# Direct DMAs of a sliding-window copy: cut into 32 KB rows mostly while the staging ring loads, left at 64 KB rows mostly while it stores

## Chip, cores, metric

One core of one Trainium2 chip. The metric is device time in microseconds (us) of one execution; lower is better. Before the change: 752.56 us, the median of 3 runs (752.02 to 753.11).

## The reference

```python
batch, length, dim = (32, 4096, 256)          # x, float32
window_size, stride = 64, 32
n_windows = (length - window_size) // stride + 1        # 127
for i in range(n_windows):
    start = i * stride
    result[:, i] = x[:, start:start + window_size].copy()
```

This is a pure copy. A block of 32 rows of x is 32 KB. A window is two neighbouring blocks, 64 KB, and each block goes to two windows, once as second half and once as first half. The output is 266 MB.

## The kernel before

There are two ways to copy a batch, and each has its own DMA queue. *Direct* batches (21 of 32) go from DRAM to DRAM on the queue of the sync engine. *Staged* batches (11) are loaded into SBUF once and stored from there twice, on the queue of the scalar engine. A staged batch reads each byte of x once instead of twice, which spares the memory, but moves 12 MB through the DMA engines where a direct one moves 8.

```python
DIRECT, IN, OUT = 32768, 16384, 16384          # largest row of a DMA descriptor, bytes
# ... in class Copier:
    def windows(self, q, b, w0, n, half=None):     # n windows of batch b, whole or one half of each
        blk = self.blk                             # 8192 elements, 32 KB
        size = 2 * blk if half is None else blk
        off = blk if half else 0
        self.count(q.dma_start(
            out=self.oap((b * self.nw + w0) * 2 * blk + off, [[2 * blk, n], [1, size]]),
            in_=bass.AP(self.x.tensor, self.x.offset + (b * self.nb + w0) * blk + off,
                        [[blk, n], [1, size]]),
            max_dma_last_dim=DIRECT))
# ... in class Staging: 6 buffers; 6 loads, their 12 stores, 5 loads, their stores
    def run(self, q):
        bufs = len(self.tiles)
        for first in range(0, len(self.batches), bufs):
            group = range(first, min(first + bufs, len(self.batches)))
            for g in group:
                self.load(q, g)
            for g in group:
                self.store(q, g)
# ... in the kernel:
    staged = [*range(1, B - 3, 3), B - 2]
    direct = [b for b in range(B) if b not in staged]
    spilled = staged[:-1]      # their full stores also write one window of each neighbour batch
    def rest(b):               # that window and 14 more, again, after those stores ("repair")
        for n in (b - 1, b + 1):
            if n in spilled:
                st.wait_stored(ring_d, spilled.index(n))
        c.windows(ring_d, b, 0 if b - 1 in spilled else 112, 15)
    # ...
        late = 8
        for i, b in enumerate(direct):
            w0 = 15 if b - 1 in spilled else 0
            for j in range(7):
                if j % 3 == 1 or (j == 3 and i % 5 != 2):
                    c.windows(ring_d, b, w0 + 16 * j, 16, 0)     # "cut": two DMAs of 32 KB rows
                    c.windows(ring_d, b, w0 + 16 * j, 16, 1)
                else:
                    c.windows(ring_d, b, w0 + 16 * j, 16)        # "whole": one DMA of 64 KB rows
            if b in free:
                rest(b)
            elif i >= len(free) + late:
                rest(direct[i - late])
        for b in direct[-late:]:
            rest(b)
```

A "slot" below is one step of the loop over j: 16 windows, 1 MB. There are 147 slots, of which 59 are cut before the change. `free` holds the one direct batch (31) that has no spilled neighbour.

Of the kernel before, what the change touches and what calls it, by code (L numbers as in the profile page):

```python
# [1 line left out]

# [4 lines left out]


DIRECT, IN, OUT = 32768, 16384, 16384


class Copier:


    def __init__(self, nc, tc, x, out, B, L, D, W, S, n_win):
        assert W == 2 * S and L % S == 0
        self.nc, self.tc, self.x, self.out = nc, tc, x, out
        self.B = B
        self.blk = S * D
        self.nb = L // S  # L20
        self.nw = n_win
        self.total = 0
        self.done = tc.alloc_semaphore("done")

    def xap(self, block, dims):
        return bass.AP(self.x.tensor, self.x.offset + block * self.blk, dims)

    def oap(self, elem, dims):
        return bass.AP(self.out.tensor, self.out.offset + elem, dims)

    def count(self, dma):
        dma.then_inc(self.done, 16)
        self.total += 16

    def windows(self, q, b, w0, n, half=None):

        blk = self.blk
        size = 2 * blk if half is None else blk
        off = blk if half else 0
        self.count(  # L40
            q.dma_start(
                out=self.oap((b * self.nw + w0) * 2 * blk + off, [[2 * blk, n], [1, size]]),
                in_=bass.AP(
                    self.x.tensor,
                    self.x.offset + (b * self.nb + w0) * blk + off,
                    [[blk, n], [1, size]],
                ),
                max_dma_last_dim=DIRECT,
            )
        )  # L50

    def load(self, q, t, b):
        return q.dma_start(
            out=t[:, :], in_=self.xap(b * self.nb, [[self.blk, self.nb], [1, self.blk]]),
            max_dma_last_dim=IN,
        )

    def store(self, q, t, b, half, p0=0, n=None):



        blk = self.blk
        n = self.nb if n is None else n
        w = b * self.nw + p0 - half
        return q.dma_start(
            out=self.oap(w * 2 * blk + half * blk, [[2 * blk, n], [1, blk]]),
            in_=t[p0 : p0 + n, :],
            max_dma_last_dim=OUT,
        )


class Staging:


    def __init__(self, c, pool, dtype, batches, bufs):
        self.c, self.batches = c, batches
        self.tiles = [pool.tile([128, c.blk], dtype, name=f"xb{i}") for i in range(bufs)]
        self.loaded = [c.tc.alloc_semaphore(f"loaded{i}") for i in range(bufs)]
        self.stored = [c.tc.alloc_semaphore(f"stored{i}") for i in range(bufs)]

    def load(self, q, g):
        n, i = divmod(g, len(self.tiles))
        if n:
            q.wait_ge(self.stored[i], 32 * n)
        self.c.load(q, self.tiles[i], self.batches[g]).then_inc(self.loaded[i], 16)

    def store(self, q, g):
        n, i = divmod(g, len(self.tiles))
        q.wait_ge(self.loaded[i], 16 * (n + 1))
        if g == len(self.batches) - 1:  # L90

            for half, p0, rows in ((0, 0, 112), (0, 112, 15), (1, 1, 15), (1, 16, 112)):
                self.c.count(self.c.store(q, self.tiles[i], self.batches[g], half, p0, rows))
            return
        for half in (0, 1):
            self.c.store(q, self.tiles[i], self.batches[g], half).then_inc(self.stored[i], 16)

    def wait_stored(self, q, g):
        n, i = divmod(g, len(self.tiles))
        q.wait_ge(self.stored[i], 32 * (n + 1))  # L100
# [11 lines that stand above are left out]
@with_exitstack  # L112
def kernel(
    ctx: ExitStack,
    tc: tile.TileContext,
    x: bass.AP,
    window_size: bass.AP,
    stride: bass.AP,
    out: bass.AP,
):  # L120
    nc = tc.nc
    W, S = int(window_size), int(stride)
    B, L, D = x.shape
    n_win = (L - W) // S + 1
    assert out.shape == (B, n_win, W, D)
    c = Copier(nc, tc, x, out, B, L, D, W, S, n_win)
    staged = [*range(1, B - 3, 3), B - 2]
    direct = [b for b in range(B) if b not in staged]
    pool = ctx.enter_context(tc.tile_pool(name="xb", bufs=1))
    st = Staging(c, pool, x.dtype, staged, 6)  # L130
    ring_d, ring_s = nc.sync, nc.scalar
    spilled = staged[:-1]

    def rest(b):
# [6 lines that stand above are left out]
    with tc.tile_critical():  # L141
        st.run(ring_s)



        free = [b for b in direct if b - 1 not in spilled and b + 1 not in spilled]
        direct = free + [b for b in direct if b not in free]
        late = 8
        for i, b in enumerate(direct):
            w0 = 15 if b - 1 in spilled else 0  # L150
            for j in range(7):
                if j % 3 == 1 or (j == 3 and i % 5 != 2):
                    c.windows(ring_d, b, w0 + 16 * j, 16, 0)
                    c.windows(ring_d, b, w0 + 16 * j, 16, 1)
                else:
                    c.windows(ring_d, b, w0 + 16 * j, 16)
            if b in free:
                rest(b)
            elif i >= len(free) + late:
# [3 lines that stand above are left out]
        ring_d.wait_ge(c.done, c.total)  # L163


# [1 line left out]
_INS = ['x', 'window_size', 'stride']  # L167
_OUTS = [((32, 127, 64, 256), 'float32')]

_NUMBERS = {'window_size': 64, 'stride': 32}  # L170


# [26 lines left out]
```

## Time and profile before

| | before |
|---|---|
| median time | 752.56 us |
| span of the profiled run | 751.0 us |
| DMA engines busy, mean of 16 | 99.3% |
| moved by the DMA engines | 313.16 MB, 417 GB/s |
| memory read + written | 220.92 + 266.99 MB, 650 GB/s |

The page of the kernel before. The DMA line is the busy share in tenths of the 16 DMA engines in 40 equal slices of the span; the next line is the rate in those slices. Of the two queues, q1 is the direct one and q10 the staging one; the columns are packets, MB, and the time that their packets took as a share of 16 engines' span.

```profile
DMA  9999999999999999999999999999999999999996
GB/s 373 418 413 428 407 419 424 428 427 428 428 427 427 426 430 422 428 417 428 421 428 403 413 423 421 421 425 418 423 427 418 428 414 427 414 433 420 416 398 293
...
q1 hardware_dynamic: 8945, 174.80, 55.1%
q10 hardware_dynamic: 9002, 138.35, 44.2%
...
HBM read 220.92 MB, written 266.99 MB: 650 GB/s over the span
```

There is no compute to speak of and no idle time: 55.1% and 44.2% are 99.3% of all engines' time. When the engines are always busy, only three things can make the kernel faster: fewer bytes, packets that take less time, or no idle engine at the end.

The packet records of the trace say how long one transfer takes. This is a count over them, not a view of the profile. A completion is the 4-byte write by which one engine reports that its part of a DMA is done:

```
before            packets   median ns   sum per engine, us   above the median, us
q1, 32 KB            5334        1213                411.6                    7.2
q10, 16 KB           8444         611                331.6                    9.2
completions, 4 B     4169           9                  2.4                      -
```

Three quarters of the data packets take exactly the median, 27 bytes per ns on either queue, so I call it the floor. The last column is what packets slower than the floor cost an engine on average, called "excess" below: 16.4 of 751 us.

The waits of the sync queue (us in total, times, longest):

```profile
SPq L41 <- DMA out_dram<-xb: 56.0, 2, 41.5
```

These are the repairs, which wait for staging's stores. They cost nothing as long as the queue has work already issued.

### The profile page before, as it was taken

What the parts mean: (1) busy time and instruction counts of PE and PEld (TensorE: products, weight loads), DVE (VectorE), ACT (ScalarE), POOL (GpSimd) and SP (SyncE); (2) the same over time, 40 slices, a digit from 0 to 9 for tenths busy, and PEclk for the clock granted to TensorE, in tenths of its full rate; (3) what the DMA queues carried; (4) which work ended last, traced back from release to release, by engine and by line L of the source; (5) the groups of instructions that cost most, each with busy time, mean ns of one, the idle gap of its engine ahead of it and who ended that gap; (6) DMA issues with size and microseconds to landing.
All of it is one profiled execution on the core that took longest, in us unless ns stands there. A gap on an engine that the chain in (4) does not pass through costs nothing. (4 is left out here: it accounts for less than half of the span.)

```text
span 751.0 us, 312 instructions
## 1 busy us (share of the span) xinstructions
POOL 0.2 (0%) x4
## 2 busy tenths in 40 slices
POOL 0000000000000000000000000000000000000000
DMA  9999999999999999999999999999999999999996
GB/s 373 418 413 428 407 419 424 428 427 428 428 427 427 426 430 422 428 417 428 421 428 403 413 423 421 421 425 418 423 427 418 428 414 427 414 433 420 416 398 293
DMA packets 17949, 313.16 MB, mean 417 GB/s; under 512 B 4169, under 2 KB 4169, under 8 KB 4169
## 3 DMA queue, kind: packets, MB, share of 16 engines
q1 hardware_dynamic: 8945, 174.80, 55.1%
q10 hardware_dynamic: 9002, 138.35, 44.2%
q14 instruction: 2, 0.02, 0.0%
HBM read 220.92 MB, written 266.99 MB: 650 GB/s over the span
## 5 line engine op out<-in xcount | busy, mean ns | idle before, releaser
L180 POOL MEMSET const-bfloat16-1.0<- 128x1 bf16 x1 | 0.1, 102 | 0.0
L180 POOL MEMSET const-uint8-127<- 128x1 uint8 x1 | 0.1, 102 | 0.0
L180 POOL MEMSET const-float32-1.0<- 128x1 f32 x1 | 0.1, 99 | 0.0
L180 POOL MEMSET const-float32-0.0<- 128x1 f32 x1 | 0.1, 98 | 0.2 <-issue 0.2
## 6 DMA issues: line engine op xcount, KB each, us to landing
out_dram<-in_x_dram SPq DMA_DIRECT2D x88, 1024.0 KB, 95.8
out_dram<-xb ACTq DMA_DIRECT2D x20, 4096.0 KB, 138.5
out_dram<-in_x_dram SPq DMA_DIRECT2D x118, 512.0 KB, 95.0
xb<-in_x_dram ACTq DMA_DIRECT2D x11, 4096.0 KB, 133.6
out_dram<-in_x_dram SPq DMA_DIRECT2D x21, 960.0 KB, 96.3
out_dram<-xb ACTq DMA_DIRECT2D x2, 3584.0 KB, 96.7
out_dram<-xb ACTq DMA_DIRECT2D x2, 480.0 KB, 96.4
```

The costliest lines, as they stand in the source:

```text
L180: nc = _bacc.Bacc("TRN2", target_bir_lowering=False, num_devices=1)
```

## The change

The diff spreads the cuts unevenly. It counts "turns" (packets and completions of the direct queue on one engine) to estimate what the staging ring is doing. Of the slots that meet loads it cuts 5 in 6, of the others 1 in 6.

```diff
--- before.py
+++ after.py
@@ -146,14 +146,21 @@
         free = [b for b in direct if b - 1 not in spilled and b + 1 not in spilled]
         direct = free + [b for b in direct if b not in free]
         late = 8
+        share = turns = 0
         for i, b in enumerate(direct):
             w0 = 15 if b - 1 in spilled else 0
             for j in range(7):
-                if j % 3 == 1 or (j == 3 and i % 5 != 2):
+                loading = turns < 102 or 306 <= turns < 391
+                share += 5 if loading else 1
+                cut = share >= 6
+                turns += 4 if cut else 3
+                if cut:
+                    share -= 6
                     c.windows(ring_d, b, w0 + 16 * j, 16, 0)
                     c.windows(ring_d, b, w0 + 16 * j, 16, 1)
                 else:
                     c.windows(ring_d, b, w0 + 16 * j, 16)
+            turns += 3 if b in free or i >= len(free) + late else 0
             if b in free:
                 rest(b)
             elif i >= len(free) + late:
```

The intent: where the two queues alternate, a cut slot brings one completion more and with it one more turn for staging. So loads should get through faster beside cut rows, and the direct queue should catch up while staging stores. The changed kernel has 55 cut and 92 whole slots.

## The prediction

> **What bounds the kernel now.** No compute: the page lists four memsets, 0.2 us. Its 40 slices show the DMA engines at 9 tenths or more until the last slice (6 tenths). In its queue part, the direct queue (q1, DRAM to DRAM) takes 55.1% and the staging queue (q10, loads to SBUF and stores from it) 44.2% of 16 engines' span: 99.3%. Packet records of the trace: direct rows of 64 KB and of 32 KB all travel as 32 KB packets, median 1213 ns (5334 of them); staging packets are 16 KB, median 611 ns (8444); a completion write takes 9 ns. That is 27.0 and 26.8 bytes per ns: a byte has one price on both queues. Sums per engine: 411.6 + 331.6 us and 2.4 us of completions. The 15-row DMAs miss one engine (21 x 2 packets x 1.213 = 51 us), so the other 15 are busy 745.7 + 51/16 = 748.9 us of the 749.3 at which the last packet ends: no idle time to win. Only 16 us per engine lie above the floor (every packet at its median): packets slowed by contention.
>
> **What the change does.** Bytes, data packets and each engine's share stay. The queues seem to alternate packet by packet on an engine, a completion write being a turn: an uncut window DMA is 3 turns, a cut pair 4. Cutting only sets how many staging packets pass per direct megabyte. Before, 59 of 147 slots are cut, spread evenly; after, 55 (built order), 5 in 6 while staging loads, 1 in 6 while it stores. Removed: 4 completions, 0.04 us. Turns stay balanced (563 before, 559 after, staging about 549). Moved: loads get a larger share (the sixth landed at 137 us; I expect near 129), stores a smaller one, so the refill starts at nearly the old time.
>
> **Waits.** The sync queue waits twice for spilled stores before repair DMAs (waits view: 56.0 us, longest 41.5). With stores slower late, I expect 55 to 65 us, longest about 47. Some 95 us of work lies in the ring (issue to landing 95.8 us), so it doesn't run dry; if it did, staging alone would fill the engines: its first packets, alone, follow each other at 616 ns.
>
> **Critical path.** The engines' total work is the path, and none of it is removed. What can move is contention: staging's part is densest while loads run (3.3 of its 9.2 us in the first 125 us, more from 400 to 525). More cut rows beside loads may move this by 1 to 3 us either way. The Trainium skill, "DMA: Bandwidth & Descriptors", section "Issuing engines are not separate DMA queues", says that DMAs from several engines run on the same 16 and interleave; this trace agrees (two queues, 99.3%).
>
> **Predicted:** 752.0 us, 748 to 756 in 8 of 10; faster by over 2%: 0.02; within 2%: 0.95; slower by over 2%: 0.03.
>
> **Right or wrong would show in:** packet medians 1213 and 611 ns unchanged; queue shares 55 and 44%; the direct queue's rate lower during loads, higher during stores; the sixth load landing earlier; last direct packet near 749 us.
>
> **What would make it wrong:** 32 KB rows at 64 KB pitch contending more with loads than whole rows do; the direct queue running dry in a repair wait while staging also waits; arbitration that isn't turn by turn, so that the queues' ends separate and a tail on one queue runs slower.

## More of the kernel before

The views by stretch give the last column in GB/s and the DMA share before it (a packet is counted where it starts, so 1.01 can occur). The stretches are chosen after the staging ring: it loads in 25 to 125 and 425 to 525 us, and stores in 125 to 400 and 525 to 650.

```profile
25.00:125.00 100.00, 0.00 (x0) 1.00 1.01 420
125.00:400.00 275.00, 0.00 (x0) 1.00 1.01 425
425.00:525.00 100.00, 0.00 (x0) 1.00 1.00 420
525.00:650.00 125.00, 0.00 (x0) 1.00 1.01 422
730.00:740.00 10.00, 0.00 (x0) 1.00 0.93 401
```

Near the end the share is 0.93, close to 15/16: one engine seems to have finished, since the 21 DMAs of 15 rows use only 15 engines (the direct queue has 3611 completions, 227 x 16 less 21). The others stay busy to about 745 us.

## The result

The changed kernel took 752.62 us (median of 4, 751.76 to 753.78), the kernel before 752.84 in the same rounds (median of 4, 752.02 to 754.57). The ratio is 0.9995 with a 95% interval of 0.9972 to 1.0018: the same. Ratios here are the mean time of one kernel's fast runs over that of the other's of the same rounds, so not quite the ratio of the quoted medians. The kernel before differed from call to call (near 745 us in some, 753 to 755 in others, at full granted clock), so only runs of one call are compared by time.

The page of the changed kernel, as above:

```profile
DMA  9999999999999999999999999999999999999997
GB/s 372 422 419 432 424 435 427 414 426 416 416 425 422 423 424 416 422 421 420 421 421 395 424 423 424 431 429 417 429 416 414 416 422 425 417 429 420 417 393 302
...
q1 hardware_dynamic: 8881, 174.80, 55.2%
q10 hardware_dynamic: 9002, 138.35, 44.1%
...
HBM read 220.92 MB, written 266.99 MB: 649 GB/s over the span
```

The shares moved by 0.1. The stretches, as above:

```profile
25.00:125.00 100.00, 0.00 (x0) 1.00 1.01 426
125.00:400.00 275.00, 0.00 (x0) 1.00 1.00 420
425.00:525.00 100.00, 0.00 (x0) 1.00 1.01 425
525.00:650.00 125.00, 0.00 (x0) 1.00 1.01 420
730.00:740.00 10.00, 0.00 (x0) 1.00 0.94 403
```

Here is the change at work: 426 in place of 420 GB/s in the first load stage and 425 in place of 420 in the second, but 420 in place of 425 and 420 in place of 422 in the store stages. The store stages are longer, so the sum is nil. The repairs' waits grew as forecast:

```profile
SPq L41 <- DMA out_dram<-xb: 63.8, 2, 41.4
```

By the packet records, the direct queue ran at 233 GB/s before and 224 after in the first load stage, and at 237 and 240 in the first store stage. The sixth load landed at 127.8 us in place of 137.4. Floors are unchanged, 1213 and 611 ns. Total excess rose from 16.4 to 17.9 us per engine, and the profiled span from 751.0 to 752.0.

### The profile page after: what moved, and what is told of

Its sections match the earlier page's. It is cut to its first block, busy times and chain, and to the rows that moved or that the text cites. A ratio compares the mean times of both kernels' runs of the same rounds, so it can differ in the third digit from the quotient of the medians.

```text
span 752.0 us, 308 instructions
## 1 busy us (share of the span) xinstructions
POOL 0.2 (0%) x4
```

## Experiments

Theories to tell apart: **(A)** whole 64 KB rows themselves slow packets; **(B)** packets slow when the direct queue's *share* of the traffic is large, whatever its rows, since a direct byte is read and written in memory while a staging byte touches it once; **(C)** only engine time matters. A further question was how much the *balance of the two queues' ends* is worth.

### e1_all_cut and e2_no_cut: every slot cut, or none

```diff
-                if j % 3 == 1 or (j == 3 and i % 5 != 2):
+                if True:            # e1_all_cut;  e2_no_cut: if False:
```

> Every direct slot as a pair of 32 KB row DMAs (147 cut, 0 whole). Turns: 651 direct against 549 staging, so by my count staging ends about 60 us earlier than before (near 680 us) and the direct queue runs alone to the end. Theory A (the engines' work is the path and whole 64 KB rows cause the slowed packets: the direct queue's excess over its 1213 ns floor was 7.2 us per engine before, 8.7 after, densest where whole rows dominate): excess of the direct queue at most 3 us while staging runs, time 743 to 750 us if the direct queue alone also runs at its floor. Theory B (the slowing follows the load on the memory, that is the direct queue's share of the traffic, whatever its rows): as low as A while staging runs, but the tail with direct traffic alone is slowed, time 752 to 775. Theory C (neither matters, only engine time): 752 within 0.3%.

> No slot cut (147 whole). Turns: 504 direct against 549 staging: the direct queue has to wait for repairs and runs dry near 690 us, staging alone fills the engines. Theories A and B both: excess of the direct queue 10 to 13 us per engine in place of 7.2, time 754 to 760. Theory C: 752 within 0.3%.

Measured: all cut 756.75 us, ratio 1.0158 (1.0142 to 1.0173); no cut 765.17 us, ratio 1.0265 (1.0221 to 1.0308). The kernel before took 745.14 in this call. All cut, the page's rates and two stretches:

```profile
GB/s 375 431 429 431 432 430 424 430 432 432 432 433 431 432 431 430 430 431 430 424 432 431 441 431 425 429 431 430 435 431 429 439 431 425 402 399 327 335 328 219
```

```profile
100.00:640.00 540.00, 0.00 (x0) 1.00 1.01 431
680.00:735.00 55.00, 0.00 (x0) 1.00 0.94 329
```

Up to 640 us the engines run at 431 GB/s, faster than the kernel before ever does over so long a stretch. By the packet records there is next to no excess there: 1.0 us between 25 and 525 us, against 6.4 in e4_long_halves of the same call, and 10.9 and 12.9 in the two profiles of the kernel before, from other calls. Staging's last packet ends at 675 us, and then the direct queue is alone at 329 GB/s: its 32 KB packets take 1493 ns on average instead of 1213. From 650 us on this queue has 11.9 us of excess, and the tail loses more than the first part won. With no cut, excess is 24.3 us in all; staging ends last, at 760.6 us against 749.2 for the direct queue. Its excess after 650 us alone is 6.2 us. Theory C falls. My number for the direct queue's excess (10 to 13 us) missed, it was 9.0; staging's rose to 15.2.

Both runs also test the alternation. If a queue gets one packet or one completion per turn, the direct queue should move 1.09 bytes per staging byte all cut (a batch is 508 KB per engine in 31 turns; staging moves 16 packets of 16 KB and a completion in 17 turns, 15.06 KB per turn) and 1.41 with no cut (508 KB in 24 turns). Measured from 150 to 600 us: 1.08 and 1.42.

### e3_swapped: the change turned round

```diff
-                share += 5 if loading else 1
+                share += 1 if loading else 3
```

> The change turned round, with the same numbers of DMAs (92 whole, 55 cut): 1 in 6 cut while staging loads, 3 in 6 while it stores. My reading (placement does not matter to the sum): same as before within 0.3%, sixth load landing near 143 us instead of 128 after and 137 before, direct excess higher than before in the load stages and lower in the store stages. Rival (the placement has a worth that the change's gain in the load stages and loss in the store stages cancel only by chance): slower by 0.3 to 1%.

Measured: 746.86 us, ratio 1.0021 (1.0006 to 1.0036); sixth load at 142.7 us. Excess is 2.8 us in the 100 us of the first load stage and only 1.6 in the 275 us of the first store stage, where c2_after below, from another call, has 1.7 and 8.8: slowed packets sit where the direct share is large. Turned round, the change gains nothing either; it is 0.2% slower, with an interval just clear of 1. The comparison of these excesses with the kernel before stays open, since that was not profiled in this call.

### e4_long_halves: only 32 KB rows, but the shares as before

```diff
-            for j in range(7):
-                ... (cut or whole, 16 windows each)
+            for n in (32, 16, 32, 16, 16):
+                c.windows(ring_d, b, w0, n, 0)
+                c.windows(ring_d, b, w0, n, 1)
+                w0 += n
```

> Only 32 KB rows, but 64 windows of a batch as two DMAs of 32 half windows each, so that the turns stay as before (567 against 563) and with them each queue's share and end. Theory A (row shape): direct excess falls from 7.2 to at most 3 us per engine, time 745 to 749. Theory B (share of traffic): excess 6 to 8 us and time 752 within 0.3%.

Measured: 746.85 us, ratio 1.0024 (1.0009 to 1.0039). The direct queue moved 1.25 bytes per staging byte, as before (1.26). Excess of the direct queue was 4.5 us and the total 10.5, the same as e3_swapped's 10.3. No row is whole, and yet no time is gained: theory A falls and B is left. The excess itself lay under B's 6 to 8; it is lower in both profiles of this call. The four profiles of the call support B in the first store stage (125 to 400 us): 1.07, 1.22, 1.25 and 1.41 direct bytes per staging byte (e1, e3, e4, e2) go with 0.6, 1.6, 2.3 and 5.8 us of excess, and e4, with no whole row, lies between the others. The share is not all: in e4's first load stage 1.22 goes with 2.2 us in only 100 us.

### c1_before and c2_after: both kernels again

The edit is a comment.

> The kernel before, unchanged but for a comment: a control, for a profile of it on the chip of these runs, since the runs of the last call were on a chip where the kernel before took 745 us and not 752. Expected: equal to before within 0.3%; excess of all packets over their floors per engine (16.4 us in its first profile) tells how far this figure differs from chip to chip. If it is the chip's own, it falls where the time falls: 10 us on a chip at 745, 16 us on one at 752.

> The changed kernel again, unchanged but for a comment. Expected: same as before within 0.3%. If the two stages' opposite shifts are real, its excess against c1_before is lower in the load stages (25 to 125 us: 1.5 against 3.1 us of both queues in the first two profiles) and higher in the store stages (125 to 400 us: 7.1 against 4.2 us).

Measured: c1_before 754.10 us (one run; the runs of before in this call had a median of 754.89); c2_after 756.06 us, ratio 1.0021 (1.0008 to 1.0034). The stretches of c1_before, then of c2_after:

```profile
25.00:125.00 100.00, 0.00 (x0) 1.00 1.01 416
125.00:400.00 275.00, 0.00 (x0) 1.00 1.01 424
425.00:525.00 100.00, 0.00 (x0) 1.00 1.00 418
525.00:650.00 125.00, 0.00 (x0) 1.00 1.01 423
```

```profile
25.00:125.00 100.00, 0.00 (x0) 1.00 1.01 425
125.00:400.00 275.00, 0.00 (x0) 1.00 1.01 418
425.00:525.00 100.00, 0.00 (x0) 1.00 1.01 427
525.00:650.00 125.00, 0.00 (x0) 1.00 1.00 417
```

The pattern repeats: plus 9 GB/s in both load stages, minus 6 in both store stages. The excess, per engine and both queues, from the packet records:

```
us            load 25-125  store 125-400  load 400-525  store 525-650    total
before               3.1            4.2           3.7            2.9      16.4
after                1.5            7.1           2.9            3.7      17.9
c1_before            3.8            5.0           4.1            3.0      18.7
c2_after             1.7            8.8           2.6            4.3      19.7
```

In the second pair the load stages win 3.6 us and the store stages lose 5.0. That is where the change's gain went. The interval of c2_after lies just above 1, so the change may cost some 0.2% there; the first comparison (0.9972 to 1.0018) does not show it.

### e5_loads_half and e6_stores_half: one half of the change alone

```diff
-                share += 5 if loading else 1
-                cut = share >= 6             # and share -= 6
+                share += 25 if loading else 12      # e6_stores_half: 12 if loading else 5
+                cut = share >= 30            # and share -= 30
```

> Only the load half of the change: 5 in 6 cut while staging loads, 2 in 5 as before while it stores (78 cut in all). Turns 582 direct against 549 staging, 19 more than before, so the direct queue is alone at the end for some 20 us more. Balance theory (a direct queue alone moves 32 KB in about 1490 ns instead of 1213, as in e1_all_cut's tail): 1 to 5 us slower than before, although its load stages have less excess. Rival (less contention beside loads is what counts): 1 to 3 us faster.

> Only the store half: 2 in 5 cut while staging loads, 1 in 6 while it stores (36 cut in all). Turns 540 direct against 549 staging: the sync queue waits longer for the repairs (75 to 110 us in all) and staging ends last. Balance theory: 1 to 6 us slower than before. Rival (a faster direct queue beside stores is what counts): 1 to 3 us faster.

Measured, in the call of the controls: loads half 757.93 us, ratio 1.0043 (1.0024 to 1.0061); stores half 761.07, ratio 1.0089 (1.0066 to 1.0113). Neither half is faster. The loads half kept the gain beside the loads (excess 1.8 us in 25 to 125, against 3.8 in the control), but staging ended 24 us before the direct queue (728.4 and 752.6). Its stretches, the last with the direct queue alone:

```profile
25.00:125.00 100.00, 0.00 (x0) 1.00 1.01 424
690.00:720.00 30.00, 0.00 (x0) 1.00 0.97 409
730.00:745.00 15.00, 0.00 (x0) 1.00 0.92 321
```

409 GB/s fall to 321. The stores half ends the other way round (direct 746.2, staging 758.5). Its waits and stretches, the last with staging alone:

```profile
SPq L41 <- DMA out_dram<-xb: 95.9, 3, 44.1
```

```profile
690.00:720.00 30.00, 0.00 (x0) 1.00 0.99 418
745.00:750.00 5.00, 0.00 (x0) 1.00 0.98 354
```

418 GB/s fall to 354. That is not what staging alone always does. In e2_no_cut it was alone as well, from 715 us on:

```profile
715.00:722.50 7.50, 0.00 (x0) 1.00 0.94 402
725.00:735.00 10.00, 0.00 (x0) 1.00 0.95 305
```

In the first stretch all 184 packets took 611 ns: ordinary stores of 128 rows, alone, stay at the floor. Counted back from the end, the slow stretch lies wholly in the stores of the last staged batch, which go in pieces of 112 and 15 rows, and so do the slow ends of e6_stores_half and, with two such batches, e9_twelve_staged. Why these are slow when alone was not tested. The direct queue alone was slow in e1_all_cut, in e5_loads_half and in e8b_no_staging, as long as most engines had work.

The profiled runs (for e5 the fastest of its six) split the difference in span from c1_before into three parts:

```
us                excess to 650 us   excess after   span less excess    span
c2_after                      +1.1           -0.2               +0.9    +1.8
e5_loads_half                 -3.4           +3.1               +2.1    +1.9
e6_stores_half                +4.7           +1.2               +1.9    +7.8
```

So the loads half did win beside the loads and lost it again at the uneven end, as the balance theory says; a loads half with even ends was not tried. The stores half lost more to slowed packets in its stages, where nothing paid for the larger direct share beside stores, than at its end: the balance theory names only the smaller part of that loss.

### e7_ten_staged: less work for the engines, more for the memory

```diff
-    staged = [*range(1, B - 3, 3), B - 2]
+    staged = [*range(1, B - 6, 3), B - 2]
-            for j in range(7):
-                ... (cut or whole, 16 windows each)
+            for n in (32, 16, 16, 16, 16, 16) if i % 2 else (32, 16, 32, 16, 16):
+                c.windows(ring_d, b, w0, n)
+                w0 += n
```

> An attempt at a version that beats both: ten batches staged instead of eleven, and whole rows in DMAs of 32 and of 16 windows so that the turns balance (495 direct against 498 staging). A staged batch costs an engine 48 x 0.611 = 29.3 us and a direct one 8 x 2.43 = 19.4 us, so the engines' floor falls by 9.9 us, 1.3%; memory traffic grows from 488 to 492 MB and the direct queue's share of the moment with it. If the engines alone limit: 742 to 747 where before takes 752 to 755. If the memory limits at about 670 GB/s, as the direct queue alone in e1_all_cut suggests (2 x 334): 735 us at the least, and the excess of packets rises from 16 to 19 us to 25 us and more, so the time is within 1% of before. I expect the latter: 745 to 757.

Measured: 764.38 us, ratio 1.0139 (1.0120 to 1.0157); I had expected 757 at most. Lines of its page:

```profile
q1 hardware_dynamic: 7854, 183.12, 58.0%
q10 hardware_dynamic: 8186, 125.77, 40.8%
...
HBM read 225.05 MB, written 266.93 MB: 644 GB/s over the span
```

4 MB less went through the engines, and it still took longer. Excess doubled, to 36.3 us, with the direct queue moving 1.52 bytes per staging byte. That is about 18 to 20 us more than in the profiles of the kernel before and of its control, taken in other calls at a similar time, and uses up the 9.9 us saved and most of the 11.5 lost; the queues also ended 9 us apart (752.9 and 762.0). All rows are whole here, so this is not the tenth batch alone.

### e8_no_staging and e8b_no_staging: the direct queue by itself

```diff
-    staged = [*range(1, B - 3, 3), B - 2]
+    staged = []
-        for b in direct[-late:]:
+        for b in []:
```

The first build (e8_no_staging) wrote eight repairs twice. The mended one ran.

> All 32 batches direct, nothing staged, each window written once, to measure the limit by itself (the first build of it wrote eight repairs twice and was refused). By the engines' floor alone: 32 x 8 x 2.43 = 622 us. By a memory ceiling of about 668 GB/s (read plus written, twice the 334 that the direct queue alone moved in e1_all_cut's tail): 532.7 MB / 668 = 797 us, with 32 KB packets near 1500 ns over the whole span. I expect 780 to 815.

Measured: 809.67 us, ratio 1.0861 (1.0844 to 1.0877). Lines of its page:

```profile
GB/s 310 331 332 329 331 336 328 329 339 329 337 336 332 326 341 329 332 313 337 328 347 334 329 331 331 337 329 337 324 334 332 334 332 332 332 331 331 329 328 259
...
q1 hardware_dynamic: 13632, 266.36, 98.5%
...
HBM read 266.34 MB, written 266.34 MB: 659 GB/s over the span
```

Engines full with 98.5% of direct packets move no more than 332 GB/s in the middle, 664 of memory traffic; the median packet takes 1541 ns in place of 1213. The floor of 622 us is out of reach. This is what staging is for. (The 334 GB/s of these expectations for e1_all_cut's tail is a little high: the view gives 329.) That the memory is the limit here is argued, not shown: a limit of DRAM-to-DRAM packets on one queue would look alike, and direct copies on two queues were not tried. Two things speak for the memory: a queue alone is not slow as such (staging in e2_no_cut, above), and the mix comes to a like sum. Moved bytes, with direct bytes counted twice, give 671 GB/s in the first store stage of e2_no_cut and 660 in that of e7_ten_staged.

### e9_twelve_staged: one more staged batch

```diff
-        if g == len(self.batches) - 1:
+        if g >= len(self.batches) - 2:
-    staged = [*range(1, B - 3, 3), B - 2]
+    staged = [*range(1, B - 3, 3), B - 2, B - 1]
-    spilled = staged[:-1]
+    spilled = staged[:-2]
-                if j % 3 == 1 or (j == 3 and i % 5 != 2):
+                if (5 * (7 * i + j)) % 7 < 5:
```

> The opposite of the ten staged: twelve batches staged (the last one too), 100 of 140 direct slots cut, so that the turns balance (580 direct, 588 staging) with a smaller direct share throughout. The engines' floor rises by 9.9 us to 742.6; memory traffic falls from 488 to 484 MB. If slowed packets follow the direct share as e1_all_cut (nearly none until its tail) and e7_ten_staged (36 us) showed, their excess falls from 16 to 19 us to 3 to 8 us and the time is within 0.7% of before: eleven staged is near the optimum, and the two ceilings trade one for one. If the excess stays near 16: 760 to 765. If it vanishes: 747 to 749, better than both.

Measured: 756.45 us (753.58 to 757.12), ratio 1.0143 (1.0123 to 1.0163): slower than I expected. The profiled run was the fastest of the five. Two stretches of it:

```profile
25.00:700.00 675.00, 0.00 (x0) 1.00 1.01 429
730.00:745.00 15.00, 0.00 (x0) 1.00 0.94 334
```

Excess fell to 7.6 us as expected. Of those, 4.7 lie after 650 us, 2.6 of them after 727.5, where staging was left alone (its last packet ended at 750.2, the direct queue's at 730.2). The build also stores two batches in pieces of 112 and 15 rows, where the others store one. In this call the kernel before took 745 us, so it cannot have had the 16 to 19 us of excess that I set out to save; at e3's and e4's 10 us, the 9.9 us of added engine work could not come back.

### What adds up

Span minus excess should be the engines' fixed work, if the reading is right:

```
us                 span   excess   difference   direct / staging end
before            751.0     16.4        734.6          749.3 / 745.7
after             752.0     17.9        734.1          750.2 / 750.2
c1_before         752.3     18.7        733.6          750.7 / 747.1
c2_after          754.1     19.7        734.4          752.3 / 752.3
e3_swapped        745.5     10.3        735.2          743.6 / 743.6
e4_long_halves    744.7     10.5        734.2          743.1 / 734.7
e9_twelve_staged  751.8      7.6        744.2          750.2 / 730.2
```

For all balanced kernels with eleven staged batches the difference is 733.6 to 735.2 us, whatever their cuts; with twelve it is 744.2, which is 9.8 us above their mean of 734.4, near the 9.9 us by which the engine work was counted to differ. So the differences in time among these are excess. This is bookkeeping: it shows that engines that are always busy lose time only by slower packets, not why packets are slow. Where the queues end apart, the difference is larger (e5 735.7, e6 735.5, e2 737.9, e1 739.5), as engines stand idle at the end. No version here beats the kernel before.

## Why the prediction was right

- **The bound.** Right: the engines' work is fixed, and the change removes four completions. The table above shows it.
- **Alternation by turns.** Right: the two extremes gave 1.08 and 1.42 bytes per staging byte against 1.09 and 1.41 counted. The sixth load was forecast near 129 us and landed at 127.8; the refill's first load was issued at 291.9 us in place of 292.9.
- **Waits.** The total was right (63.8 us in the range 55 to 65). The longest was forecast at 47 and stayed 41.4.
- **The end.** Both queues still end together, at 750.2 us, as the balance of turns said.
- **The level.** Partly luck: 752.0 is what the kernel before took when the forecast was made. The scored call was like that one; in the later call c2_after took 756.06, outside the range, and the kernel before itself lay between 745 and 755. What the mechanism forecast is the ratio, near 1, and that held in both calls.
- **Contention.** Right in size (total excess up by 1.5 us, and 1.0 in the repeat), but I looked for movement beside loads only. The step that was incomplete: slowed packets follow the direct queue's share in the store stages too, so what was won in one stage was given back in the other. That the two cancel so nearly was not forecast.
- **"A byte has one price on both queues."** True of the median while both run. The direct queue alone takes 1493 ns and not 1213 for 32 KB, and its median is 1541 with no staging at all.
- **"If it did, staging alone would fill the engines."** Right for ordinary stores: alone, they moved 402 GB/s in e2_no_cut with every packet at 611 ns. Wrong for the stores of the last batch: 354 GB/s in e6_stores_half and 334 in e9_twelve_staged. It did not matter, since the queue did not run dry.

The page "DMA: Bandwidth & Descriptors" of the Trainium skill says, under "Queues, rings and completion order", that each DMA engine round-robins between the queue rows that have work. The measured byte ratios agree with that. What stays open is why direct packets are slowed, why the kernel before takes 745 us in one call and 753 in another, and whether its own excess explains that, since no profile of it was taken in a call at 745. The record lists chip 4 both for e7's call (752.92 us) and for that of e8b and e9 (745.28), so the chip's number alone does not tell.

## What to carry to other kernels

When two queues keep all DMA engines busy and move a fixed number of bytes, changing who goes first in which stage can move slowed packets about without removing them, as here. Look first at whether both queues end together, since the direct queue alone moved about a quarter less here than the two mixed (329 against 431 GB/s), and judge a shift of shares by the excess over the packet's floor, stage by stage. A mix that spares a second limit (here probably memory, by staging) has an optimum, and one batch more or less staged cost 1.4% on either side here, though part of one of the two was a tail, and both also changed the cuts.

## What the Trainium skill lacked or had wrong

- "DMA: Bandwidth & Descriptors", "Queues, rings and completion order", gives a turn of the round robin as a packet of about 9 to 17 descriptors. Here the byte ratios fit a turn of one 32 KB or 16 KB transfer record (the trace does not count its descriptors), and a 4-byte completion, though it takes 9 ns, used up a whole turn: 1.08 against 1.42 bytes per staging byte, with the same data transfers.
- "HBM Reference", "Specifications (TRN2)", says that a core streaming alone measures about 425 GB/s, bounded by its 16 DMA engines. The mixed traffic agrees (417 GB/s). It lacks DRAM-to-DRAM copies, which use the memory twice: 332 GB/s moved, 664 read plus written, under the page's 716 GB/s per domain. The only rates for such copies that I found are in "DMA: Bandwidth & Descriptors", "Latency and other measured facts", in a row on row pitch: up to 214 GB/s per direction, called full, for tiles of 16 KiB rows. The rows here are longer, and moved 332.
- "DMA: Bandwidth & Descriptors", "Specifications", gives about 27 GiB/s (29 GB/s) for one engine. Measured, when nothing slows a packet: 32 KB in 1213 ns, 27.0 GB/s, which is 432 GB/s for 16 engines and fits the same table's 435 better.
- I found no page with a rate for stores of 112 or 15 rows from SBUF: as the last batch, alone, they moved 305 to 354 GB/s in three runs, against 402 GB/s for stores of 128 rows alone.
